# One level of Strassen's scheme in the up-projection of a hybrid decoder step

## The chip, the cores and the metric

The kernel runs on one core of one Trainium2 chip. The metric is the time of one execution on the device, in microseconds (us). A core has five engines that work through their own instruction lists in order and wait for each other by semaphores: TensorE (PE in the profile, with its weight loads as PEld), VectorE (DVE), ScalarE (ACT), GpSimd (POOL) and SyncE (SP), which here issues most DMAs. Matmul results land in eight PSUM banks.

## The reference

One inference step of a decoder layer for 1024 prompt tokens and 64 sample tokens (8 sequences of 8), width 1024, all in float32. A mixer with two branches (a gated linear recurrence and a retention) adds to `x`; then comes the part that the change is in:

```python
    x = x + merged @ w_o
    up = _rmsnorm(x, g_ffn) @ w_up                     # 1024 -> 6144
    upc, conv_ffn_new = _causal_dwconv(up, conv_ffn0, w_ffn_conv, b_ffn_conv)
    gate, val = upc[..., :D_FF], upc[..., D_FF:]       # D_FF = 3072
    x = x + (jax.nn.gelu(gate) * val) @ w_down
    e = _rmsnorm(p.astype(x.dtype) @ w_ple, g_ple)
    x = x + jax.nn.sigmoid(x @ w_ple_gate) * e
```

The convolution has width 3 over time. A last normalisation follows. The outputs are `x` of all tokens and the new states.

## The kernel before, in words

**Halves and units.** The tokens are worked through in two halves, one after the other: the first holds 512 prompt tokens, the second 512 prompt and the 64 sample tokens (576). Rows are kept with channels on partitions and tokens along the free dimension, eight rows of 128 channels for width 1024. The weights of all projections are packed in DRAM as units of 128 x 1024 numbers (512 KB): one unit holds the weights from 1024 inputs to 128 outputs, as eight blocks of 128 x 128. `unit_order` (L58) writes the order of all 330 units by hand; `dense` (L300) and `unit` (L245) run one.

**Two parts.** For precision each operand is split into a float32r part and the exact rest. `block` (L233) does three matmuls for a block: high by high, high by low, low by high; in the second half each of them for two groups of 288 columns, in the first for one of 512. So a unit is 24 matmuls of 512 or 48 of 288. The weights' split is `split_hi` (L224, a cast on ScalarE) and `split_lo` (L228, a subtraction on VectorE); rows are split by `pair` (L306).

**The weight stream.** While unit i runs, its block 0 issues the cast of unit i+2, block 2 the subtraction of i+2, and block 3 the load of unit i+4 by SP (two raw buffers, three buffers for each part).

**Jobs and ticks.** All other work is written as generators. After each block `tick` (L201) advances every job: a job that yields n goes on n ticks later. This fixes the program order of every engine; nothing is reordered later. A result that is asked for with `need` before its job is done makes the job run to its end at once.

**The feed-forward before.** The eight `wo` units add to the residual rows; `j_wo` (L975) splits the rows times `g_ffn` straight away, without the norm. Then for f in 0 to 23 come the up unit of the gate, the up unit of the value and, from f = 4 on, one down unit. The norm of the tokens is found meanwhile by `stat` (L357): sums of squares by small matmuls (L365), a power on GpSimd (L375), a diagonal on VectorE (L380, L390), a broadcast by matmul (L399) and a copy (L400). It is multiplied in when a result is taken out of PSUM (`evac_flat`, L411). `conv` (L436) does one tap on ScalarE (L441) and two on VectorE (L445); then gelu (L991), product (L999) and split. The down units run in groups of four f's: one adds into two residual rows. After the 24 f's come two units of the per-layer embedding (`ple`), whose squares are added up on GpSimd (L354) at once, then the last four down units, then eight gate units and the final normalisation; the second half's input is prepared beside the first half's gate units.

Of the kernel before, what the change touches and what calls it, by code (L numbers as in the profile page):

```python
# [22 lines left out]
RAW = 2  # L23
WIDE = 12
NROW = 70
# [11 lines left out]
# per-channel parameters, one column per 128 channels  # L37
# [4 lines left out]
# constants that depend on shapes alone  # L42
# [15 lines left out]
def unit_order(hf):  # L58
# [8 lines left out]
    for f in range(FF):  # L67
        o += [("up", f), ("up", FF + f)]
        if f >= GRP:
            o.append(("down", f - GRP))  # L70
    o += [("ple", 0), ("ple", 1)]
    o += [("down", f) for f in range(FF - GRP, FF)]
    o += [("gate", m) for m in range(8)] * (1 + hf)
    return o


ORDER = unit_order(0) + unit_order(1)
NU = len(ORDER)
PACKED = unit_order(0)
# [46 lines left out]
class Trunk:  # L126
    def __init__(self, ctx, tc, io):
# [35 lines left out]
        self.cur = 0  # L163
        self.phase = ""
        self.low, self.forced = {}, {}

# [1 line left out]
    def new(self, n=None, dt=F32, wide=False):  # L168
        if n is not None:
            return [self.new(dt=dt, wide=wide) for _ in range(n)]  # L170
        i = (self.wide if wide or not self.free else self.free).popleft()
# [14 lines left out]
    def ps_new(self, n):  # L186
        return [self.banks.popleft() for _ in range(n)]
# [32 lines left out]
    def load(self, i):  # L220
        if i < NU:
            self.nc.sync.dma_start(self.raw[i % RAW], self.io["wpk"][WHERE[ORDER[i]]])

# [21 lines left out]
    def unit(self, H, what, specs, after=None, groups=None):  # L245
        i = self.begin(what)
        for b, (ps, xp, start, stop) in enumerate(specs):
# [5 lines left out]
            if b == 0:  # L253
                self.split_hi(i + 2)
            if b == 2:
                self.split_lo(i + 2)
            if b == 3:
                self.load(i + 4)

    def first_units(self, H, xn, w):  # L260
        """the first two units side by side, at the pace of the arriving input."""
        i = [self.begin(("lx", m)) for m in range(2)]
        ps = [self.ps_new(H.G) for _ in range(2)]
        for k in range(8):
# [4 lines left out]
            if k == 0:  # L269
                self.split_hi(2)  # L270
                self.split_lo(2)
                self.load(4)
            if k == 1:
                self.split_hi(3)
                self.split_lo(3)
                self.load(5)
# [3 lines left out]
    def gates_abreast(self, x2p, groups):  # L280
        """the first two gate units; the block that reads the newest rows comes last in both."""
        i = [self.begin(("gate", m)) for m in range(2)]
        ps = [self.ps_new(len(groups)) for _ in range(2)]
        for m, k in [(m, k) for m in range(2) for k in range(7)] + [(0, 7), (1, 7)]:
# [3 lines left out]
            if m == 0 and k == 0:  # L288
                self.split_hi(i[0] + 2)
            if m == 0 and k == 2:  # L290
                self.split_lo(i[0] + 2)
            if m == 0 and k == 3:
                self.load(i[0] + 4)
            if m == 0 and k == 7:
                self.split_hi(i[1] + 2)
                self.split_lo(i[1] + 2)
                self.load(i[1] + 4)
# [8 lines left out]
    def pair(self, H, row, keep=False):  # L306
        """row -> its float32r part and the exact rest."""
# [34 lines left out]
    def square(self, x, ssum, m, eng=None):  # L342
        """ssum += x * x; with an engine of its own the last square is returned instead."""
# [13 lines left out]
    def stat(self, chunks, ssum, slot, after=None):  # L357
        """1 / sqrt(mean of squares + eps) of every token, on all partitions; ssum: rows to be added up."""
# [52 lines left out]
    def evac_flat(self, H, ps, xf, rb, w):  # L411
        """xf <- ps * rb in the layout of the causal convolution: each sequence after its own prefix."""
# [23 lines left out]
    def conv(self, H, xf, w, wcol, bcol, out=None):  # L436
        """causal depthwise convolution; the last tap writes `out` (compact) when given."""
# [51 lines left out]
    def p0(self, H, xn):  # L489
        """the scaled input in two parts; returns the normalisation of the tokens."""  # L490
# [196 lines left out]
    def back(self, on, h0, np_, t0, ogn):  # L687
        """token-major -> channels on partitions, with the norm's own scale and shift."""
# [16 lines left out]
    def masked_q(self, q, ch, n):  # L705
        """queries of a pair of heads, each with the other's rows at zero."""
# [216 lines left out]
    def branch(self, H, xn, rb, ga, ya, src, lead, m1=None, hook=None):  # L923
        """sigmoid(gate) * projection of src; plus m1 and split when m1 is given."""
# [50 lines left out]
    def j_wo(self, H, ps, x, ssum, m):  # L975
        self.add_ps(H, x, ps)
        yield 1
        p = yield from self.pair_scaled(H, x, self.v("g_ffn", m))
        yield from self.square(x[:, 0:H.T], ssum[:, 0:H.T], m)
        return p  # L980

    def j_up(self, H, u, ps, xf, rb):
        self.evac_flat(H, ps, xf, self.need(rb), 2)
        yield 1
# [9 lines left out]
    def j_val(self, H, up, gate):  # L994
        t, n = yield from up
# [15 lines left out]
    def down(self, H, i, hp, x1):  # L1011
        g, j = divmod(i, GRP)
        ps = [self.ps_new(H.G), self.ps_new(H.G)]
        out = []

        def ev(mi):
            out.append(self.start(self.j_down(H, ps[mi], x1[2 * j + mi], g == FF // GRP - 1)))

        self.unit(
            H, ("down", i), [(ps[mi], hp[GRP * g + kk], kk == 0, kk == 3) for mi in range(2) for kk in range(4)],  # L1020
            {3: lambda: ev(0), 7: lambda: ev(1)},
        )
        if j == GRP - 1:
            for kk in range(GRP):
                self.rel(hp.pop(GRP * g + kk))
        return out

    def j_ple(self, H, ps, e, ssum, m):
        self.act_ps(H, e, ps, AF.Copy)
        yield 1  # L1030
        yield from self.square(e[:, 0:H.T], ssum[:, 0:H.T], m)

    def j_embed(self, H, pe, ssum):
        yield 6
        rb = yield from self.stat(H.chunks, [ssum], H.hf)
        yield 2
        for m in range(8):
            self.nc.vector.scalar_tensor_tensor(
                pe[m][:, 0:H.T], pe[m][:, 0:H.T], self.v("g_ple", m), rb[:, 0:H.T], op0=ALU.mult, op1=ALU.mult
            )  # L1040
            yield 2
# [17 lines left out]
    def j_final(self, H, g, x3, outs, ssum, slot, last):  # L1059
        """the last normalisation of the tokens of g, and the store."""  # L1060
# [29 lines left out]
    def run(self, H, res, nxt):  # L1090
# [17 lines left out]
        # rotary queries and keys  # L1108
# [15 lines left out]
        # values, token-major  # L1124
        self.phase = f"{H.hf} v"
        vt = [self.new(2) for _ in H.chunks]
        for g in range(4):
            banks = self.ps_new(len(H.chunks))
            for j in range(2):
                i = self.begin(("v", 2 * g + j))  # L1130
                wh, wl = (w[i % RING].rearrange("p a b -> p (a b)") for w in (self.whi, self.wlo))
                for c, (t0, nt) in enumerate(H.chunks):
# [9 lines left out]
                    if c == 0:  # L1142
                        self.split_hi(i + 2)
                    if c == 1:
                        self.split_lo(i + 2)
                        self.load(i + 4)
# [6 lines left out]
        # LRU output gate  # L1153
# [12 lines left out]
        # retention beside its gate  # L1166
# [16 lines left out]
        # output projection  # L1183
# [10 lines left out]
        x1p = []  # L1194
        for m in range(8):
            if m + 3 < 8:
                xload(m + 3)
            ps = self.dense(H, ("wo", m), mg)
            x1p.append(self.start(self.j_wo(H, ps, xr[m], ssum, m)))
        x1 = [xr[m] for m in range(8)]  # L1200
        self.rel(mg)

        def stat2():
            yield 7
            for j in x1p:
                self.need(j)
            return (yield from self.stat(H.chunks, [ssum], H.hf))

        rb2 = self.start(stat2())
        # gated convolutional feed-forward  # L1210
        self.phase = f"{H.hf} ffn"
        pp = []
# [8 lines left out]
        hp = {}  # L1221
        gate = None
        for f in range(FF):
            if f == FF - 1:
                pp = [self.start(j_p(kk), delay=kk) for kk in range(2)]
            for s in range(2):
                u = s * FF + f
                xf = self.new(wide=True)
                self.prefix(H, xf, self.stf[:, u], 2)
                ps = self.dense(H, ("up", u), x1p)  # L1230
                up = self.j_up(H, u, ps, xf, rb2)
                late = 8 if f == 0 and s == 0 else 0
                if s == 0:
                    gate = self.start(self.j_gelu(H, up), delay=late)
                else:
                    hp[f] = self.start(self.j_val(H, up, gate), delay=late)
            if f >= GRP:
                self.down(H, f - GRP, hp, x1)
        # per-layer embedding
        self.phase = f"{H.hf} ple"  # L1240
        pe, jp = [], []
        ssum = self.new()
        for j in range(2):
            ps = [self.ps_new(H.G) for _ in range(4)]

            def ev(mi):
                e = self.new()
                pe.append(e)
                jp.append(self.start(self.j_ple(H, ps[mi], e, ssum, 4 * j + mi)))

            self.unit(
                H, ("ple", j), [(ps[mi], pp[kk], kk == 0, kk == 1) for mi in range(4) for kk in range(2)],
                {2 * mi + 1: (lambda mi=mi: ev(mi)) for mi in range(4)},
            )
        self.rel(pp, x1p, rb2)

        emb = self.start(self.j_embed(H, pe, ssum))
# [324 lines left out]
```

## Time and profile before

| | before |
|---|---|
| runs (3) | 2098.27 to 2098.78 us, median 2098.53 |
| span of the profiled execution | 2098.5 us |
| first half's feed-forward, 510.88 to 877.59 | 366.7 us |
| second half's feed-forward, 1568.14 to 2009.30 | 441.2 us |
| granted TensorE clock, mean of the core | 0.996 |
| HBM read, written | 193.95 MB, 7.67 MB |

In the profile's groups a row reads: line of the code, engine, operation, output <- inputs by the program's names, shape, count, then busy us and mean ns of one, then the idle time of the engine just before them and who ended it. In the timeline a row reads start, length, engine, line, operation. In the chain of work in order of time: start, length, engine and line, and how many instructions are merged. The borders of the two stages in the table are where, in that chain, the unbroken TensorE work of the feed-forward begins and ends.

### The profile page before, as it was taken

The page shows a single profiled execution, that of the slowest core. Times are in us where ns is not written, and L with a number is a line of the kernel's source. Part 1 is how long each engine was busy: PE and PEld are TensorE (multiplying, and loading weights), DVE is VectorE, ACT ScalarE, POOL GpSimd, SP SyncE. Part 2 cuts the span into 40 slices and gives each one's busy share as a digit, 9 for nine tenths or more (in the row PEclk, how much of TensorE's full clock was granted, in tenths as well). Part 3 has the DMA queues.
Part 4 walks back from the last instruction along what each step waited for, and adds up shares of the span by engine and source line. Part 5 has one row for each costly group of instructions (what it writes and reads, how often), then busy time and mean ns, then how long its engine had stood idle before and what let it go on. Part 6 is the DMA issues. An engine that isn't in the chain of part 4 may idle for free.

```text
span 2098.5 us, 31597 instructions
## 1 busy us (share of the span) xinstructions
PE 2072.7 (99%) x12862; PEld 1903.0 (91%) x12862; DVE 1274.8 (61%) x1944; ACT 811.0 (39%) x1150; POOL 387.0 (18%) x608
## 2 busy tenths in 40 slices
PE   9999999999999999998999999999999999999997
PEld 7798888888888888888999999989999999999997
DVE  7965345655766666588884433544447556555667
ACT  5654233434433333454463322333234333332354
POOL 4640013102000000234541001440030000000022
PEclk9999999999999999999999999999999999999998
DMA  5333321343333332343332222222322222222234
GB/s 194 98 104 91 101 81 51 101 123 99 100 101 101 91 101 91 111 146 88 117 96 81 83 89 61 94 88 81 116 91 81 84 88 81 81 81 91 84 100 145
DMA packets 64082, 203.67 MB, mean 97 GB/s; under 512 B 7488, under 2 KB 9920, under 8 KB 63936
## 3 DMA queue, kind: packets, MB, share of 16 engines
q1 hardware_dynamic: 63072, 200.97, 31.0%
q8 instruction: 101, 1.65, 0.3%
q10 hardware_dynamic: 864, 0.68, 0.1%
q14 instruction: 45, 0.37, 0.1%
HBM read 193.95 MB, written 7.67 MB: 96 GB/s over the span
## 4 chain that ended last, share of the span: by engine, by line
PE 68%; DVE 4%; issue 2%; ACT 1%; POOL 0%; DMA 0%; DVEq 0%; SPq 0%; ACTq 0%; POOLq 0%
PE bank L237 62%; PE bank L1138 1%; PE bank L1139 1%; PE bank L1137 1%; DVE wlo L231 1%; DVE row L445 0%; DVE row L312 0%; PE bank L883 0%; PE bank L872 0%; DVE row L1053 0%; POOL row L354 0%; PE bank L769 0%; PE bank L767 0%; PE bank L779 0%; PE bank L745 0%
## 5 line engine op out<-in xcount | busy, mean ns | idle before, releaser
L237 PE MATMUL bank<-row,whi 128*128 128x288 f32 (+3 forms) x7360 | 1627.5, 329 | 0.0
L237 PEld LDWEIGHTS bank<-row,whi 128*128 128x128 f32 x7360 | 1185.1, 189 | 97.4 <-issue 0.9
L237 PE MATMUL bank<-row,wlo 128*128 128x288 f32 (+3 forms) x3680 | 1013.4, 327 | 0.8 <-DVE wlo L231 0.7
L237 PEld LDWEIGHTS bank<-row,wlo 128*128 128x128 f32 x3680 | 628.7, 189 | 49.6 <-DVE wlo L231 1.4
L231 DVE TENSOR_TENSOR wlo<-raw,whi 128x1024 fp32r<-128x1024 f32 x330 | 427.1, 1294 | 133.6 <-ACT whi L226 132.3
L226 ACT CAST whi<-raw 128x1024 fp32r<-128x1024 f32 x330 | 344.0, 1042 | 225.6 <-PE bank L237 128.7
L441 ACT ACTIVATE row<-row,vec 128x512 f32<-128x512 f32 (+2 forms) x112 | 95.0, 850 | 397.9 <-DVE row L419 228.9
L445 DVE SCALAR_TENSOR_TENSOR row<-row,vec,row 128x512 f32<-128x512 f32 (+2 forms) x224 | 182.9, 817 | 99.0 <-ACT row L441 95.0
L329 DVE TENSOR_TENSOR row<-bank,row 128x288 f32<-128x288 f32 (+1 forms) x144 | 72.5, 531 | 172.7 <-PE bank L237 172.7
L432 POOL COPY stf<-row 128x2 f32<-128x2 f32 x96 | 18.3, 191 | 740.3 <-DVE row L419 393.6
L354 POOL TENSOR_TENSOR row<-row,row 128x512 f32<-128x512 f32 (+2 forms) x49 | 79.2, 1619 | 359.0 <-ACT row L350 351.0
L310 ACT CAST row<-row 128x512 fp32r<-128x512 f32 (+1 forms) x132 | 84.8, 647 | 150.4 <-DVE row L999 72.6
L312 DVE TENSOR_TENSOR row<-row,row 128x512 fp32r<-128x512 f32 (+1 forms) x132 | 98.1, 745 | 24.1 <-ACT row L310 23.2
L334 DVE TENSOR_TENSOR row<-bank,row 128x288 f32<-128x288 f32 (+1 forms) x168 | 84.0, 528 | 36.2 <-PE bank L237 36.2
L417 DVE TENSOR_TENSOR row<-bank,row 128x288 f32<-128x288 f32 x56 | 25.5, 456 | 113.2 <-PE bank L237 110.6
L415 DVE TENSOR_TENSOR row<-bank,row 128x512 f32<-128x512 f32 x56 | 38.5, 690 | 80.7 <-PE bank L237 78.9
L711 POOL TENSOR_TENSOR row<-row,cst 128x256 f32<-128x256 f32 (+1 forms) x36 | 25.0, 725 | 315.0 <-PE bank L237 315.0
L1138 PE MATMUL bank<-wlo,row 128*128 128x256 f32 (+1 forms) x288 | 81.4, 283 | 0.0
L1139 PE MATMUL bank<-whi,row 128*128 128x256 f32 (+1 forms) x288 | 81.4, 283 | 0.0
L1137 PE MATMUL bank<-whi,row 128*128 128x256 f32 (+1 forms) x288 | 81.4, 282 | 0.0
L909 ACT ACTIVATE row<-row 128x512 f32<-128x512 f32 (+1 forms) x32 | 21.1, 659 | 135.7 <-DVE row L329 135.7
L1137 PEld LDWEIGHTS bank<-whi,row 128*128 128x128 f32 (+1 forms) x288 | 53.3, 185 | 0.0
(156 smaller groups left out, 1418.5 us busy)
## 6 DMA issues: line engine op xcount, KB each, us to landing
raw<-wpk SPq DMA_DIRECT2D x330, 512.0 KB, 3.6
row<-xB SPq DMA_DIRECT2D x16, 288.0 KB, 4.2
row<-xA SPq DMA_DIRECT2D x16, 256.0 KB, 5.3
row<-tabB SPq DMA_DIRECT2D x8, 288.0 KB, 4.7
row<-wri SPq DMA_DIRECT2D x8, 256.0 KB, 5.4
row<-tabA SPq DMA_DIRECT2D x8, 256.0 KB, 4.1
yA<-row SPq DMA_DIRECT2D x8, 256.0 KB, 3.6
row<-s SPq DMA_DIRECT2D x8, 256.0 KB, 6.1
```

Of the source, the lines that this page charges most:

```text
L226: self.nc.scalar.copy(self.whi[i % RING], self.raw[i % RAW])
L231: self.nc.vector.tensor_sub(self.wlo[j], self.raw[i % RAW], self.whi[j].bitcast(F32))
L237: self.nc.tensor.matmul(b[:, 0:g.stop - g.start], lhsT=w, rhs=x[:, g], start=s, stop=e)
L310: nc.scalar.copy(hi[:, 0:H.T], row[:, 0:H.T])
L312: nc.vector.tensor_sub(lo[:, 0:H.T], row[:, 0:H.T], hi[:, 0:H.T].bitcast(F32))
L334: self.nc.vector.tensor_add(row[:, g], b[:, 0:H.n], row[:, g])
L354: (eng or nc.gpsimd).tensor_add(ssum, ssum, s[:, 0:n])
L441: nc.scalar.activation(t[:, 0:n], xf[:, 0:n], AF.Identity, bias=bcol, scale=wcol(0))
L445: nc.vector.scalar_tensor_tensor(t[:, 0:n], xf[:, j:j + n], wcol(j), t[:, 0:n], op0=ALU.mult, op1=ALU.add)
L1137: nc.tensor.matmul(b, lhsT=xh, rhs=wh[:, ws], start=j == 0 and kk == 0, stop=False)
L1138: nc.tensor.matmul(b, lhsT=xh, rhs=wl[:, ws], start=False, stop=False)
L1139: nc.tensor.matmul(b, lhsT=xl, rhs=wh[:, ws], start=False, stop=j == 1 and kk == 3)
```

## The change

The product of the up-projection is cut in two along each dimension, and the eight half-size products become seven. In the weights (A) the first index is gate or value, the second the half of the 1024 inputs; in the rows (B) the first index is the half of the inputs, the second the half of the tokens. The weights' sums are s1 = a21 + a22, s2 = a11 + s1, s3 = a11 + a21, s4 = a12 + s2. The rows' are t1 = b11 - b12, t2 = -t1 - b22, t3 = b22 - b12, t4 = b21 + t2. The signs that this leaves are put right when the products are taken out of PSUM.

- The four sums of weights do not come from the host. During the first half's mixer `make_sums` copies halves of units from DRAM to DRAM by SP and adds to them with accumulating DMAs by GpSimd, four f's at a time.
- The weight stream takes two halves of 128 x 512 as one slot of eight blocks. A product for one f is four blocks, a `step`. There are 84 slots for 24 f's in a half of the tokens where there were 48 units. Three raw buffers now, loads five units ahead.
- `operands` normalises the residual rows first, and splits the rows and their eight differences.
- `step` runs a product and takes its result out of PSUM: products 1 and 2, and 3 and 5, share a bank.
- The first six f's run product by product, all others f by f; 19 of 24 down units run inside the stage and 5 behind it.
- The two embedding units run before the feed-forward; their rows wait in DRAM, and squares and norm of them come beside the last down units.
- `new` and `ps_new` tick the jobs until a row or a bank is free.

```diff
+PRODUCTS = {
+    1: ("a11", "b11"), 2: ("a12", "b21"), 3: ("s4", "b22"), 4: ("a22", "t4"),
+    5: ("s1", "t1"), 6: ("s2", "t2"), 7: ("s3", "t3"),
+}
+def ffn_plan():
+    plan = [("step", f, p) for p in (1, 2, 6, 7, 5, 4, 3) for f in range(LEADP)]      # LEADP = 6
+    steps, down = len(plan), 0
+    for f in range(LEADP, FF):
+        todo = [(f, 1), (f, 6)] + [(f - 1, 3)] * (f > LEADP) + [(f, p) for p in (7, 5, 4, 2)]
+        ready = min(f - 4, down + 2)
+        for i, x in enumerate(todo):
+            plan.append(("step", *x))
+            steps += 1
+            while i >= len(todo) - 2 and steps % 2 == 0 and down < ready:
+                plan.append(("down", down))
+                down += 1
+    plan.append(("step", FF - 1, 3))
...
+    def make_sums(self):
+        yield 30
...
+        for c in range(FF // CHUNK):                                                  # CHUNK = 4
+            for name, base in (("s1", "a21"), ("s3", "a11"), ("s2", "a11"), ("s4", "a12")):
+                nc.sync.dma_start(dst(c, name), src(c, base))
+                yield 7
+            yield 8
+            for name, more in (("s1", "a22"), ("s3", "a21"), ("s2", "s1"), ("s4", "s2")):
+                nc.gpsimd.dma_start(dst(c, name), dst(c, more) if more in SUMS else src(c, more), accum_op=ALU.add)
+                yield 14
+    def hook(self, i, b):
+        if b == 0:
+            self.split_hi(i + 2)
+        if b == 2:
+            self.split_lo(i + 2)
+        if b == 3:
+            self.load(i + 5)
...
+    def operands(self, H, x1, ssum, sq, X, held):
...
+        yield 3
+        rb = yield from self.stat(H.chunks, [ssum] + [r for r in (self.need(j) for j in sq) if r is not None], H.hf)
...
+        def split(row, names):
+            hi, lo = self.new(2, F32R)
+            nc.scalar.copy(hi[:, 0:T], row[:, 0:T])
+            nc.vector.tensor_sub(lo[:, 0:T], row[:, 0:T], hi[:, 0:T].bitcast(F32))
...
+        for k in range(4):
+            norm(k)
+            r = self.new(dt=F32R)
+            nc.scalar.copy(r[:, h1], xn[k][:, h1])
+            nc.vector.tensor_sub(r[:, h2], xn[k][:, h1], r[:, h1].bitcast(F32))
+            yield 0.5
+        for k in range(4, 8):
+            norm(k)
+            split(xn[k], ("b21", "b22"))
+            yield 1
...
+        for k in range(4):
+            t = self.new()
+            nc.vector.tensor_sub(t[:, h1], xn[k][:, h1], xn[k][:, h2])
+            nc.vector.scalar_tensor_tensor(t[:, h2], t[:, h1], -1.0, xn[4 + k][:, h2], op0=ALU.mult, op1=ALU.subtract)
+            split(t, ("t1", "t2"))
+            yield 1
+        for k in range(4):
+            t = self.new()
+            nc.vector.tensor_sub(t[:, h1], xn[4 + k][:, h2], xn[k][:, h2])
+            nc.vector.tensor_add(t[:, h2], xn[4 + k][:, h1], ts[k][:, h2])
+            split(t, ("t3", "t4"))
+            yield 1
...
+    def step(self, H, X, prep, P, f, p):
...
+        for kk in range(4):
+            b = 4 * h + kk
...
+            mm(out, lhsT=wh, rhs=xh, start=first and kk == 0, stop=False, skip_group_check=True)
+            mm(out, lhsT=wh, rhs=xl, start=False, stop=False, skip_group_check=True)
+            mm(out, lhsT=wl, rhs=xh, start=False, stop=kk == 3, skip_group_check=True)
+            if kk % 2:
+                self.tick()
+            self.hook(i, b)
+        if p == 1:
+            nc.scalar.copy(s["row"][:, 0:n], out)
...
+        if p == 2:
+            nc.scalar.copy(s["xg"][:, 2:2 + n], out)
+        elif p == 6:
+            V.tensor_add(r2, out, r1)
+        elif p == 7:
+            V.tensor_add(r1, out, r2)
+        elif p == 5:
+            for o, of in self.second(H, s["xv"], 2):
+                V.scalar_tensor_tensor(o, of(bank), -1.0, of(r1), op0=ALU.mult, op1=ALU.subtract)
+        elif p == 4:
+            V.tensor_sub(s["xv"][:, 2:2 + n], out, r1)
+            s["val"] = self.start(self.j_conv(H, FF + f, s["xv"]), delay=1)
+        else:
+            for o, of in self.second(H, s["xg"], 2):
+                V.tensor_add(o, of(bank), of(r2))
+            gate = self.start(self.j_gelu(H, self.j_conv(H, f, s["xg"])), delay=1)
+            s["hp"] = self.start(self.j_val(H, s["val"], gate), delay=6)
```

In the second half of the tokens the pieces that `second` names are two, the prompt's and the sample's, so those evictions take two instructions.

More of the change, by code (lines that the diff above doesn't have):

```diff
@@ L22 @@
 RING = 3
-RAW = 2
-WIDE = 12
-NROW = 70
+RAW = 3
+WIDE = 16
+NROW = 68
+LEADP = 6
 LEAD_A, LEAD_B = 2, 4
@@ L163, in __init__ @@
         self.cur = 0
+        self.half = None
+        dram = ctx.enter_context(tc.tile_pool(name="sums", bufs=1, space=bass.MemoryType.DRAM))
+        self.sums = [dram.tile([128, CHUNK, len(SUMS), 512], F32, name=f"sums{i}") for i in range(FF // CHUNK)]
+        self.embed = [dram.tile([128, 8, 576], F32, name=f"embed{i}") for i in range(2)]
         self.phase = ""
@@ L170, in new @@
             return [self.new(dt=dt, wide=wide) for _ in range(n)]
+        for _ in range(400):
+            if self.wide or (self.free and not wide):
+                break
+            self.tick()
         i = (self.wide if wide or not self.free else self.free).popleft()
@@ L186, in ps_new @@
     def ps_new(self, n):
+        for _ in range(400):
+            if len(self.banks) >= n:
+                break
+            self.tick()
         return [self.banks.popleft() for _ in range(n)]
@@ L992, in j_gelu, with j_val @@
         return t
-    def j_val(self, H, up, gate):
-        t, n = yield from up
+    def j_val(self, H, val, gate):
+        t, n = self.need(val)
         g = self.need(gate)
@@ L1193, in run @@
         ssum = self.new()
[L1194 to L1212, printed above, removed]
+        sq = []
         srcp = self.io["pA"] if H.hf == 0 else self.io["pB"]
@@ L1219, in j_p @@
             return (yield from self.pair(H, p))
[L1221 to L1238, printed above, removed]
+        pp = [self.start(j_p(kk), delay=8 + kk) for kk in range(2)]
@@ L1257, in run @@
-        emb = self.start(self.j_embed(H, pe, ssum))
+            i = self.begin(("ple", j))
+            for mi in range(4):
+                ps = self.ps_new(H.G)
+                for kk in range(2):
+                    b = 2 * mi + kk
+                    self.block(H.groups, ps, self.whi[i % RING][:, b], self.wlo[i % RING][:, b], self.need(pp[kk]), kk == 0, kk == 1)
+                    self.tick()
+                    self.hook(i, b)
+                self.start(self.j_ple(H, ps, 4 * j + mi))
@@ L1258, in run @@
+        self.rel(pp)
+        self.phase = f"{H.hf} ffn"
+        P = {}
+        for what, *x in PLAN:
+            if what == "step":
+                self.step(H, X, prep, P, *x)
+            else:
+                self.down(H, *x, P, x1)
+        self.rel(held)
+        pe = []
+        emb = self.start(self.j_embed(H, pe))
         x2p = []
-        for f in range(FF - GRP, FF):
-            x2p += self.down(H, f, hp, x1)
+        for d in range(DOWNS, FF):
+            x2p += self.down(H, d, P, x1)
@@ L1358, in main @@
             nc.sync.dma_start(self.stl, io["stl"])
+            self.load(4)
             w_hi(0, 0)
```

230 lines of the change are left out of this document (164 added, 66 removed).

## The prediction

> **What bounds the kernel now.** I read the page first, then the windows and the chain of waits over the two feed-forward stages, then the groups by shape, then the timeline of single operations.
>
> ```profile
> span 2098.5 us, 31597 instructions
> PE 2072.7 (99%) x12862; PEld 1903.0 (91%) x12862; DVE 1274.8 (61%) x1944; ACT 811.0 (39%) x1150; POOL 387.0 (18%) x608
> ```
>
> TensorE is busy for the whole span, so what it does not have to multiply is saved, as long as it is fed. VectorE's 61% is a mean; the stage decides.
>
> ```profile
> 510.88:877.59 366.71, 366.71 (x1616) 302.92 (x1615) 237.01 (x301) 140.98 (x173) 16.07 (x94) 1.00 0.32 98
> 1568.14:2009.30 441.16, 441.16 (x3315) 441.16 (x3315) 269.05 (x464) 156.34 (x194) 39.41 (x193) 1.00 0.27 84
> 940.00:950.00 10.00, 5.65 (x24) 4.05 (x22) 9.07 (x8) 6.65 (x11) 6.36 (x3) 1.00 0.24 59
> 950.00:960.00 10.00, 8.20 (x33) 6.57 (x33) 8.16 (x15) 2.80 (x4) 6.08 (x7) 0.83 0.30 99
> 960.00:970.00 10.00, 10.00 (x61) 9.57 (x61) 3.73 (x5) 2.86 (x5) 1.79 (x2) 0.83 0.37 107
> ```
>
> Columns: stretch, length, busy time of PE, PEld, DVE, ACT, POOL, granted clock, DMA share, GB/s. The first two rows are the feed-forward of the two halves: TensorE never idles, VectorE is busy 65% and 61%. The three others, in the first half's last stage, show what an idle TensorE costs twice: it stands still for 4.35 us, and the next 20 us run at a clock of 0.83.
>
> ```profile
> 510.88 366.71 PE bank L237 x1614
> 1568.14 441.16 PE bank L237 x3312
> ```
> ```profile
> 115.68 0.28 PE L1137 MATMUL bank<-whi,row 128*128 128x256 f32 x1
> ...
> 121.31 0.28 PE L1139 MATMUL bank<-whi,row 128*128 128x256 f32 x1
> ```
>
> The chain in order of time gives the pace of matmuls: 366.71 / 1614 = 0.2272 us at 512 columns, 441.16 / 3312 = 0.1332 us at 288. The value projection shows 256 columns: its first and its 48th matmul are 5.63 us apart, 0.1198 us each. The recorded length (0.28) is not the pace.
>
> **1. Products.** Per f the two up units had 2x8x3 = 48 block matmuls per group of columns; seven products have 7x4x3 = 84 of half the tokens. First half: 48 of 512 columns, 48x0.2272 = 10.91 us, become 84 of 256, 84x0.1198 = 10.06. Second half: 96 of 288 become 84 of 288. Over 24 f: 24x0.85 = 20.2 us, and 24x12x0.1332 = 38.4 us. **Gain 58.6 us.** The first half gets little, since a matmul of 256 columns costs more than half of one of 512.
>
> The Trainium skill ("TensorE: Matmul & The Clock Gate", Back-to-back issue gap) gives columns / 2.4 + 2.5 ns, 109 and 216 ns for these two; by it, as an estimate, the first half would gain 28 us and the sum below would be 8 us lower. The rows measure both shapes in this kernel and are slower, so they are used.
>
> **2. Weight halves.** 14 half units a f make 3.5 slots of eight blocks where there were 2 units, so 36 more slots a half of tokens, each with one cast (ScalarE) and one subtraction (VectorE).
>
> ```profile
> L231 DVE TENSOR_TENSOR wlo<-raw,whi 128x1024 fp32r<-128x1024 f32 x330 | 427.1, 1294 | 133.6 <-ACT whi L226 132.3
> L445 DVE SCALAR_TENSOR_TENSOR row<-row,vec,row 128x512 f32<-128x512 f32 x112 | 89.4, 799 | 46.0 <-ACT row L441 44.0
> L445 DVE SCALAR_TENSOR_TENSOR row<-row,vec,row 128x592 f32<-128x592 f32 x96 | 80.0, 835 | 47.5 <-ACT row L441 45.8
> L312 DVE TENSOR_TENSOR row<-row,row 128x576 fp32r<-128x576 f32 x66 | 52.4, 795 | 12.0 <-ACT row L310 11.7
> L312 DVE TENSOR_TENSOR row<-row,row 128x512 fp32r<-128x512 f32 x66 | 45.8, 695 | 12.1 <-ACT row L310 11.5
> L334 DVE TENSOR_TENSOR row<-bank,row 128x288 f32<-128x288 f32 x112 | 45.7, 449 | 20.8 <-PE bank L237 20.8
> L310 ACT CAST row<-row 128x576 fp32r<-128x576 f32 x66 | 44.2, 674 | 72.8 <-DVE row L999 39.8 <-DVE row L334 18.8 <-DVE row L918 5.6
> L310 ACT CAST row<-row 128x512 fp32r<-128x512 f32 x66 | 40.7, 621 | 77.6 <-DVE row L999 32.8 <-DVE row L448 17.3 <-DVE row L334 17.1
> L334 DVE TENSOR_TENSOR row<-bank,row 128x512 f32<-128x512 f32 x56 | 38.3, 684 | 15.4 <-PE bank L237 15.4
> L1038 DVE SCALAR_TENSOR_TENSOR row<-row,vec,row 128x576 f32<-128x576 f32 x8 | 6.5, 810 | 0.0
> L1038 DVE SCALAR_TENSOR_TENSOR row<-row,vec,row 128x512 f32<-128x512 f32 x8 | 6.0, 745 | 0.0
> L350 ACT ACTIVATE row<-row 128x256 f32<-128x256 f32 x7 | 2.9, 415 | 5.0 <-DVE row L1054 5.0
> L354 DVE TENSOR_TENSOR row<-row,row 128x256 f32<-128x256 f32 x6 | 2.5, 423 | 2.1 <-ACT row L350 2.1
> ```
> ```profile
> 706.98 1.22 DVE L231 TENSOR_TENSOR wlo<-raw,whi 128x1024 fp32r<-128x1024 f32 x1
> 708.12 0.69 DVE L334 TENSOR_TENSOR row<-bank,row 128x512 f32<-128x512 f32 x1
> 708.72 0.68 DVE L312 TENSOR_TENSOR row<-row,row 128x512 fp32r<-128x512 f32 x1
> ```
>
> Back to back, VectorE starts the next instruction 0.09 us before the record of the last ends (706.98 to 708.12 is 1.14, not 1.22), so an instruction costs its length less 0.09. A plain step of f in the first half is then 4.5 subtractions x 1.14, five evictions of 256 columns (0.33, between the 288 and 512 rows), four convolution taps (0.71), product, split and two adds (0.60 each): 12.0 us of VectorE against 10.06 + 24x0.2272 = 15.5 of TensorE (second half 13 against 17.6). The middle of the stage is still TensorE's. Its two ends are not.
>
> **3. The start of the stage: the normalised operands.** Before, the matmuls ran on unnormalised rows and the eviction multiplied. Now nothing starts before the norm, and only the two embedding units cover it. They tick once a block; the job's waits put the sums of squares at tick 4, the diagonal at 7, the broadcast at 11.
>
> ```profile
> 504.44 1.05 PE bank L365 x8
> ...
> 510.42 0.47 PE bank L399 x2
> ```
> ```profile
> 1560.57 0.99 PE bank L365 x10
> ...
> 1567.34 0.80 PE bank L399 x4
> ```
>
> The sums are now of two rows, so L365 doubles to 2.1 and 2.0 us: **+2.0** in all. First half, from the start of the embedding units: 11 blocks of 0.68, 2.1, L399 and its copy 1.2: norm at 10.8 us; units done at 16x0.68 + 2.1 + 0.5 = 13.5. Second: 12.4 and 15.6.
>
> Every tick from 11 to 24 then issues operand work, eight rows to normalise and split and eight differences. In each, VectorE's subtraction stands right behind ScalarE's cast of the same row, so VectorE, in order, waits for it (0.04 to pass on). First half: four rows of b11 0.75 + 0.42 + 0.42 + 0.08 - 0.09 = 1.57; four of b2x 0.75 + 0.62 + 0.70 + 0.08 - 0.09 = 2.05; eight differences 0.42 + 0.45 (a fused one at 256, estimate from L354 and L1038) + 0.62 + 0.70 - 0.10 = 2.1. Sum 31.3 us. What is queued behind: each slot's subtraction, issued two slots ahead by program order. That of slot 2 stands behind nine rows of this, slot 3 behind thirteen, slot 4 behind all. So slot 4's weights are ready at 10.8 + 31.3 + 4x1.14 = 46.7 us, while TensorE by then has 13.5 and four slots of 24x0.1198 = 2.88, 25.0 us: a stall of 21.5 (0.24 of slot 4 runs first). Second half, same sum at 576 and 288: 1.70, 2.27 and 2.33 give 34.5; 12.4 + 34.5 + 4.6 = 51.5 against 15.6 + 4x3.2 = 28.4: 22.8. **Cost 44.3 us.** Bounds: without the waits for ScalarE the rows cost 0.99, 1.26 and 1.29 (second 1.09, 1.43, 1.47), and the stalls are 9.5 and 10.2, 19.7 in all; above, embedding evictions of 0.6 each between the casts add 5. I take the upper figure since nothing stands between cast and subtraction.
>
> These idle pieces are 5 to 7 us long, and the rows at 950 lost 20x0.17 = 3.4 us after one of 4.35. Most of a slow clock hides under VectorE; the last slot's does not: 2.5 a half, **+5** (0 to 7). The Trainium skill (same page, Why this matters for your kernels) says to leave no gap over about 3 us; the trace agrees.
>
> **4. The lead's end.** Six f's finish products 4 and 3 together, so twelve convolutions fall on six slots of TensorE. VectorE per slot, first half: 1.14 + two evictions 0.66 + two convolutions 2x1.45 = 4.7 for slots 16 to 18, then with products and splits 5.3, 6.5, 6.8, against 2.88. The subtraction for two slots on may be late by two slots before TensorE stops. Adding up, it is late by 0.3 at slot 20, 2.1, 4.6, 8.2 and 11.2 at slot 24, after which two down units (2x5.45 of TensorE, 4.8 of VectorE) win it back. Second half, per slot 5.0, 5.0, 5.1, 5.9, 7.3, 7.5 against 3.2: 11.7. **Cost 22.9** (0, if the queue's order lets it drain, to 30). ScalarE's casts in these slots sum to about the same, but follow VectorE.
>
> **5. Moves.** The embedding units cost the same earlier. Their squares (POOL, L354) now run beside five downs: L365 may wait for POOL, 1 us a half, **+2** (-3 to +8; the stall of 4.35 us above lies next to it and may shift). The base copies go through SP ahead of weight loads, the accumulating ones through POOL, which waits for each to land.
>
> ```profile
> q1 hardware_dynamic: 63072, 200.97, 31.0%
> raw<-wpk SPq DMA_DIRECT2D x330, 512.0 KB, 3.6
> ```
>
> 31% of the DMA engines moved 97 GB/s, so all move some 313. A chunk's four copies (4 MB in 28 ticks, 19 us) beside 1.9 MB of weights need 18.8 us: just enough. A load now has 2.6 units, 14.2 us, less 3.6 to land: 10.6 to spare. I take nothing, for that spare hides it; 0 to +50 with the rival below. No gain is possible here. The sums are issued by tick 30 + 6x92 = 582, their use begins at 656.
>
> **Sum.** The span is the profiled execution's own time and equals the median (2098.53) within 0.1. 2098.5 - 58.6 + 44.3 + 2.0 + 5 + 22.9 + 2 = **2116 us**.
>
> **Rivals.** (a) Faster: VectorE's queue is not the wall. If the operand rows cost only their busy time and the lead's convolutions drain into the downs, 2098.5 - 58.6 + 19.7 + 2 + 2.5 = 2064 us. It decides where an operand row takes under 1.4 us. For it: VectorE has 35% free in the stage. Against: program order. (b) One end only: the lead's convolutions drain, the operands do not: 2116 - 23 = 2093. (c) The copies starve the mixer's weights. If a byte from DRAM to DRAM costs two, six chunks need (8 + 1.9) / 0.313 = 31.6 us for 19 + 10.6, 2 late each: 2128; at 2.5 it is 2166. It decides at 1.85. For it: the bursts fill the engines. (d) The change does not save the products: excluded, the 256-column pace is in the trace.
>
> **Numbers.** Forecast 0.46, (a) 0.30, (b) 0.12, (c) 0.12. Forecast alone: 2102 to 2132, from the bounds of 4 and the clock. The range 2060 to 2138 takes in (a) and half of (c). A difference of 0.2% (4.2 us) is what can be told. Faster: (a) and half of (b), 0.36; same: the rest of (b) and the forecast's edge, 0.08; slower 0.56.
>
> **What would show it.** Right: behind each embedding stage three idle pieces of TensorE of 5 to 7 us ending on wlo, with VectorE alternating with ScalarE; two more shorter stalls on wlo 50 us later; clock under 1 there; middle of the stage at 15.5 and 17.6 us a f without waits; mixer of the first half unchanged. Wrong: TensorE unbroken behind the embedding, or waits for raw or POOL before it.

## The result, and the profile after

| | before | after |
|---|---|---|
| median of 4 runs each | 2098.46 us | 2125.43 us |
| lowest to highest | 2098.27 to 2098.78 | 2124.10 to 2125.81 |
| ratio, 95% interval | | 1.0128 (1.0114 to 1.0143) |
| span of the profiled execution | 2098.5 us | 2124.0 us |
| granted TensorE clock, mean | 0.996 | 0.982 |

The kernel is slower by 27.0 us, 9.4 more than the forecast of 2116, on the side forecast and inside the range. Between the two profiled spans it is 25.5 us.

The page of the changed kernel, to be read against the first rows of the prediction:

```profile
span 2124.0 us, 34118 instructions
PE 2046.8 (96%) x13456; PEld 1912.2 (90%) x13456; DVE 1418.7 (67%) x2176; ACT 919.6 (43%) x1334; POOL 445.5 (21%) x630
```

TensorE has less to do in spite of its slower clock (2046.8 us for 2072.7), but no longer does it without a break: 77 us of the span are idle, where 26 were.

Windows of the first half's feed-forward (stretch, length, busy time of PE, PEld, DVE, ACT, POOL, granted clock, DMA share, GB/s):

```profile
513.93:555.00 41.07, 27.47 (x145) 24.99 (x144) 27.55 (x44) 18.90 (x35) 0.00 (x0) 0.75 0.29 96
555.00:590.00 35.00, 34.12 (x282) 33.74 (x281) 25.06 (x39) 15.35 (x17) 1.11 (x6) 1.00 0.54 177
590.00:619.00 29.00, 21.73 (x156) 20.92 (x155) 28.65 (x44) 19.54 (x27) 4.39 (x7) 0.89 0.30 97
619.01:895.65 276.64, 276.64 (x1896) 258.19 (x1895) 220.01 (x313) 140.11 (x185) 25.75 (x70) 1.00 0.47 151
655.77:686.87 31.10, 31.10 (x218) 29.17 (x217) 24.76 (x36) 15.86 (x21) 2.84 (x9) 1.00 0.48 153
1751.57:1786.59 35.02, 35.02 (x267) 35.02 (x266) 27.13 (x47) 16.49 (x21) 4.24 (x17) 1.00 0.43 136
```

The lead is the first six f's, which run product by product. The first row is the stall behind the embedding units: TensorE stands for 13.6 of 41 us and runs the rest at a clock of 0.75, while VectorE, busy 67%, is not full either. That is how two engines look that wait for each other. In the third, the lead's end, VectorE is full (28.65 of 29.00). The fourth is the rest of the stage, without a gap. The last two are two f's each in the middle of the halves: 15.55 and 17.51 us a f.

TensorE's timeline in the stall, the operations with a wait of 0.4 us or more ahead of them (in brackets the wait and who ended it; L1156 to L1158 are the three matmuls of a step's block, L323 the cast and L328 the subtraction of the weights):

```profile
516.91 0.50 PE L1156 MATMUL bank<-row,whi 128*128 128x256 f32 x1 [1.73 <-ACT row L1094]
527.89 0.39 PE L1156 MATMUL bank<-row,whi 128*128 128x256 f32 x1 [2.00 <-ACT whi L323]
530.50 0.45 PE L1158 MATMUL bank<-row,wlo 128*128 128x256 f32 x1 [2.10 <-DVE wlo L328]
537.54 0.58 PE L1156 MATMUL bank<-row,whi 128*128 128x256 f32 x1 [2.66 <-ACT whi L323]
540.28 0.58 PE L1158 MATMUL bank<-row,wlo 128*128 128x256 f32 x1 [1.94 <-DVE wlo L328]
547.02 0.39 PE L1156 MATMUL bank<-row,whi 128*128 128x256 f32 x1 [2.08 <-ACT whi L323]
548.28 0.58 PE L1158 MATMUL bank<-row,wlo 128*128 128x256 f32 x1 [0.76 <-DVE wlo L328]
```

Three slots, 10 us apart, come late. Each is waited for twice: for its high part, which was not forecast, and two matmuls later for its low part.

VectorE's timeline, inside the stall:

```profile
520.88 0.75 DVE L1078 SCALAR_TENSOR_TENSOR row<-row,vec,row 128x512 f32<-128x512 f32 x1
522.36 0.69 DVE L1086 TENSOR_TENSOR row<-row,row 128x512 fp32r<-128x512 f32 x1 [0.74 <-ACT row L1085]
522.97 0.75 DVE L1078 SCALAR_TENSOR_TENSOR row<-row,vec,row 128x512 f32<-128x512 f32 x1
```

A row takes 522.97 - 520.88 = 2.09 us (2.05 forecast), of which VectorE idles 0.74 until ScalarE has cast the row.

TensorE's timeline at the lead's end, the operations with a wait of 1 us or more:

```profile
601.54 0.39 PE L1158 MATMUL bank<-row,wlo 128*128 128x256 f32 x1 [1.40 <-DVE wlo L328]
606.84 0.39 PE L1158 MATMUL bank<-row,wlo 128*128 128x256 f32 x1 [2.16 <-DVE wlo L328]
613.95 0.58 PE L1158 MATMUL bank<-row,wlo 128*128 128x256 f32 x1 [3.28 <-DVE wlo L328]
```

All three are for the low part of the weights.

### The profile page after: what moved, and what is told of

Its sections match the earlier page's. It is cut to its first block, busy times and chain, and to the rows that moved or that the text cites. A ratio compares the mean times of both kernels' runs of the same rounds, so it can differ in the third digit from the quotient of the medians.

```text
span 2124.0 us, 34118 instructions
## 1 busy us (share of the span) xinstructions
PE 2046.8 (96%) x13456; PEld 1912.2 (90%) x13456; DVE 1418.7 (67%) x2176; ACT 919.6 (43%) x1334; POOL 445.5 (21%) x630
## 4 chain that ended last, share of the span: by engine, by line
PE 79%; DVE 13%; issue 3%; ACT 3%; DMA 1%; POOL 1%; SPq 0%; DVEq 0%; ACTq 0%; POOLq 0%
PE bank L334 49%; PE bank L1158 7%; PE bank L1157 7%; PE bank L1156 7%; DVE wlo L328 3%; DVE row L532 2%; PE bank L1366 2%; PE bank L1367 2%; PE bank L1365 2%; DVE row L399 1%; ACT whi L323 1%; ACT row L1085 1%; PE bank L854 1%; PE bank L866 1%; PE bank L832 1%
## 5 line engine op out<-in xcount | busy, mean ns | idle before, releaser
L334 PE MATMUL bank<-row,whi 128*128 128x288 f32 (+3 forms) x5056 | 1126.2, 330 | 1.5 <-ACT whi L323 1.0
L334 PEld LDWEIGHTS bank<-row,whi 128*128 128x128 f32 x5056 | 815.8, 189 | 68.2 <-ACT whi L323 1.4
L334 PE MATMUL bank<-row,wlo 128*128 128x288 f32 (+3 forms) x2528 | 700.2, 328 | 4.0 <-DVE wlo L328 4.0
L328 DVE TENSOR_TENSOR wlo<-raw,whi 128x1024 fp32r<-128x1024 f32 x402 | 518.5, 1291 | 191.1 <-ACT whi L323 190.5
L323 ACT CAST whi<-raw 128x1024 fp32r<-128x1024 f32 x402 | 420.0, 1046 | 351.0 <-issue 122.8
L334 PEld LDWEIGHTS bank<-row,wlo 128*128 128x128 f32 x2528 | 434.4, 189 | 39.2 <-DVE wlo L328 5.4
L1158 PE MATMUL bank<-row,wlo 128*128 128x256 f32 (+1 forms) x1344 | 397.7, 296 | 23.7 <-DVE wlo L328 23.7
L1156 PE MATMUL bank<-row,whi 128*128 128x256 f32 (+1 forms) x1344 | 397.9, 296 | 21.8 <-ACT whi L323 16.3
L1157 PE MATMUL bank<-row,whi 128*128 128x256 f32 (+1 forms) x1344 | 397.0, 295 | 0.2
L1158 PEld LDWEIGHTS bank<-row,wlo 128*128 128x128 f32 x1344 | 263.2, 196 | 26.6 <-DVE wlo L328 26.6
L1156 PEld LDWEIGHTS bank<-row,whi 128*128 128x128 f32 x1344 | 263.0, 196 | 26.0 <-ACT whi L323 17.9
L1157 PEld LDWEIGHTS bank<-row,whi 128*128 128x128 f32 x1344 | 263.2, 196 | 2.0 <-DVE row L1095 1.3
L519 POOL COPY stf<-row 128x2 f32<-128x2 f32 x96 | 47.2, 492 | 742.7 <-DVE row L1191 450.3
L421 DVE TENSOR_TENSOR row<-bank,row 128x288 f32<-128x288 f32 (+1 forms) x168 | 81.0, 527 | 29.3 <-PE bank L334 29.3
L1367 PE MATMUL bank<-whi,row 128*128 128x256 f32 (+1 forms) x288 | 81.3, 282 | 0.0
```

What stands on the lines that cost most here:

```text
L323: self.nc.scalar.copy(self.whi[i % RING], self.raw[i % RAW])
L328: self.nc.vector.tensor_sub(self.wlo[j], self.raw[i % RAW], self.whi[j].bitcast(F32))
L334: self.nc.tensor.matmul(b[:, 0:g.stop - g.start], lhsT=w, rhs=x[:, g], start=s, stop=e)
L1156: mm(out, lhsT=wh, rhs=xh, start=first and kk == 0, stop=False, skip_group_check=True)
L1157: mm(out, lhsT=wh, rhs=xl, start=False, stop=False, skip_group_check=True)
L1158: mm(out, lhsT=wl, rhs=xh, start=False, stop=kk == 3, skip_group_check=True)
```

## The experiments

The theory: the loss is VectorE's program order at two places, the operand rows that each wait for a cast, and the lead's convolutions bunched at its end. Rivals: the sum of VectorE's work, whatever its order; the clock; the copies for the sums of weights. Medians are compared with the kernel before on the same chip: 2097.97 us (19 runs) for the first four experiments, 2098.28 (13) for the next four, 2098.50 (7) for the last two. The experiments without an interval are one run each, and runs of the kernel before on one chip lie up to 3.3 us apart.

**1. The cast one row ahead.** In `operands` each subtraction is issued one row later, so ScalarE has had a whole row's time for the cast.

```diff
+        rest = deque()
             nc.scalar.copy(hi[:, 0:T], row[:, 0:T])
-            nc.vector.tensor_sub(lo[:, 0:T], row[:, 0:T], hi[:, 0:T].bitcast(F32))
+            def low():
+                nc.vector.tensor_sub(lo[:, 0:T], row[:, 0:T], hi[:, 0:T].bitcast(F32))
...
+            rest.append(low)
...
+        def late():
+            while len(rest) > 1:
+                rest.popleft()()
```

> Only the order inside the operand work is changed: the subtraction of a row is issued one row later, so that ScalarE's cast of it has VectorE's next row to hide under. Theory (VectorE's in-order wait for the cast is what makes an operand row cost 1.6 to 2.1 us): a row falls to its busy time, 1.0 to 1.5 us, the stall behind the embedding units from 21.5 to about 9.5 us in the first half and from 22.8 to about 10.2 in the second, so 24 us less: 2101 us. Rival (VectorE's load or the weights' arrival sets the stall, the waits lie beside it): within 5 us of the changed kernel, 2120 to 2126.

Measured: 2098.17 us (10 runs), ratio to before 1.0002 (0.9993 to 1.0012), 27 us under the changed kernel. No operation was removed; what went is the wait for the cast, with what it brings along. VectorE's timeline:

```profile
517.15 0.75 DVE L1079 SCALAR_TENSOR_TENSOR row<-row,vec,row 128x512 f32<-128x512 f32 x1
517.81 0.69 DVE L1089 TENSOR_TENSOR row<-row,row 128x512 fp32r<-128x512 f32 x1
518.42 0.75 DVE L1079 SCALAR_TENSOR_TENSOR row<-row,vec,row 128x512 f32<-128x512 f32 x1
```

A row now takes 518.42 - 517.15 = 1.27 us, without a wait. Of the 29.3 us between the two profiled spans, 19.8 are idle time of TensorE. The other 9.5 are busy time, for the same matmuls at a mean clock of 0.988 instead of 0.982; 1.6 of the 29.3 arise before the value projection, where the clock held in this execution (see experiment 5). TensorE's waits, summed, are shorter for both parts of the weights; first the changed kernel, then this one (L1180 and L1178 stand for L1158 and L1156):

```profile
PE bank L1158 <- DVE wlo L328: 23.7, 12, 3.3
PE bank L1156 <- ACT whi L323: 16.3, 7, 4.4
```
```profile
PE bank L1180 <- DVE wlo L328: 16.9, 12, 3.1
PE bank L1178 <- ACT whi L323: 6.2, 4, 2.7
```

**2. The rows spread out.** From the fifth row on a row comes every third tick instead of every tick; the order inside a row stays.

```diff
-            yield 1
+            yield 3
```

> Only the yields of the operand work are changed: three ticks instead of one between rows from the fifth on, so that fewer of them stand ahead of each slot's weight subtraction. Theory (program order makes the weights of slots 2 to 4 wait behind all operand rows, but a row still costs 2.1 us): the stall then ends where the last row is needed, at product 7: about 15 us in each half instead of 21.5 and 22.8, so 14 us less, 2111. Rival (the order does not matter, the sum of the work does): 2122 to 2126.

Measured: 2104.88 us, 20.5 under the changed kernel, more than expected. So it is not VectorE's total that stops TensorE there: the same work, thinned out, lets the weights through.

**3. Both.**

> Both edits together. Theory: rows at their busy time and in step with the slots leave 2 to 3 us of stall in each half, so 39 us less than the changed kernel, and most of the loss of clock (5 us) goes too: 2081 to 2087 us, faster than the kernel before. Rival (VectorE's load in the lead is the bound): above 2100.

Measured: 2095.72 us (10 runs), ratio 0.9990 (0.9981 to 0.9999). A miss, 9 us above the expected range: the two gains do not add. VectorE's timeline shows a wait for the weights' cast that recurs with the slots (13 times from 513 to 600 us, 10.6 us in all), and ScalarE's shows why:

```profile
532.48 0.68 DVE L1089 TENSOR_TENSOR row<-row,row 128x512 fp32r<-128x512 f32 x1
534.47 1.23 DVE L328 TENSOR_TENSOR wlo<-raw,whi 128x1024 fp32r<-128x1024 f32 x1 [1.31 <-ACT whi L323]
```
```profile
532.60 0.62 ACT L1086 CAST row<-row 128x512 fp32r<-128x512 f32 x1 [1.81 <-DVE row L1126]
533.13 0.37 ACT L1194 COPY row<-bank 128x256 f32<-128x256 f32 x1
533.39 1.05 ACT L323 CAST whi<-raw 128x1024 fp32r<-128x1024 f32 x1
```

ScalarE waits 1.81 us for VectorE's difference row, with the cast of the weights queued behind that; VectorE then waits 1.31 us for this cast, with the next rows queued behind that. Block 0 issues the cast and block 2 the subtraction, too close together when an operand row falls between.

**4. The lead without its taps.**

```diff
-        for j in range(1, w + 1):
+        for j in range(1, w + 1) if taps else ():
```

> The changed kernel with the two VectorE taps of the twelve convolutions of the first six f's left out in each half of the tokens (so part of the convolution is not computed). Theory (the convolutions that pile up at the lead's end cost 11.2 and 11.7 us): 23 us less, 2102. Rival (ScalarE's casts or the banks bound that stretch): less than 8 us off, above 2117.

Measured: 2105.45 us, 20.0 under the changed kernel, against 22.9 forecast for the pile-up. The lead's convolutions do stop TensorE.

**5. No sums of weights.** Each sum is replaced by the half `a11` as it lies in DRAM.

```diff
         if name in SUMS:
-            return self.sums[f // CHUNK][:, f % CHUNK, SUMS.index(name), :]
+            name = "a11"
-            self.start(self.make_sums())
```

> The changed kernel without the DMAs that form the sums of weights (the up-projection then takes a plain half in place of each sum, so it computes something else). Theory (these DMAs hide under the mixer): the embedding units of the first half begin within 0.5 us of where they begin in the changed kernel (500.95 us), and the time stays at 2123 to 2126. Rival (copies and accumulations delay weights or GpSimd's work in the mixer): they begin 1.5 us earlier, where the kernel before has the same point, and the time falls by 1.5 us or more.

Measured: 2122.86 us, 2.6 under the changed kernel, which for one run is within the spread of runs; the trace tells more. The embedding units start 2.2 us sooner, and the rival's 1.5 was nearer. But the sums do not starve the mixer. Windows from the first value-projection matmul to the embedding units, before and after:

```profile
115.68:499.40 383.72, 383.72 (x1954) 327.75 (x1953) 199.14 (x294) 141.08 (x215) 70.37 (x62) 1.00 0.31 94
```
```profile
117.34:500.95 383.61, 383.59 (x1954) 327.87 (x1953) 198.46 (x289) 137.75 (x210) 89.61 (x81) 1.00 0.77 205
```

With the DMA engines busy 77% instead of 31%, the 384 us are the same to 0.1. The loss lies before 117 us. VectorE's groups there, 67 to 73 us, two convolution taps, first without sums and then in the changed kernel, and what GpSimd ran beside them in the latter:

```profile
L532 DVE SCALAR_TENSOR_TENSOR row<-row,vec,row 128x512 f32<-128x512 f32 x2 | 3.3, 1670 | 0.2 <-ACT row L528 0.2
```
```profile
L532 DVE SCALAR_TENSOR_TENSOR row<-row,vec,row 128x512 f32<-128x512 f32 x2 | 4.3, 2166 | 0.2 <-ACT row L528 0.2
```
```profile
69.25 1.40 POOL L309 DMA_DIRECT2D sums<-wpk  x1
70.17 1.82 POOL L643 TENSOR_TENSOR row<-row,row 128x512 f32<-128x512 f32 x1
```

The first accumulating DMA's issue occupies GpSimd for about 1 us (its next instruction starts 0.92 us later), and VectorE's two taps beside GpSimd's work, slow already without it, take 1.0 us more. TensorE then waits 1.10 us at 74.04 as well as 1.18 at 75.73, and behind these two the clock falls in some executions and not in others. Windows of the changed kernel and of experiment 1, which has the same program up to there:

```profile
75.00:80.00 5.00, 4.27 (x12) 3.41 (x13) 4.18 (x6) 2.10 (x4) 1.52 (x2) 0.67 0.80 200
```
```profile
75.00:80.00 5.00, 4.29 (x19) 3.56 (x20) 4.19 (x6) 2.09 (x4) 1.50 (x2) 1.00 0.80 197
```

At 0.67 there are 12 matmuls in the 5 us, at full clock 19. The value projection starts at 117.34 us in the first, 115.74 in the second, 115.14 without sums. So the sums cost 0.6 us, or 2.2 where the clock falls.

**6. The weights' subtraction later.** Experiment 3, and in the lead the subtraction of a slot's weights at block 6 and the load at block 7.

```diff
-        if b == 2:
+        if b == (6 if self.lead else 2):
             self.split_lo(i + 2)
-        if b == 3:
+        if b == (7 if self.lead else 3):
             self.load(i + 5)
...
+                    self.lead = LEADP not in P and x[0] < LEADP
```

> The third experiment's kernel, and in the lead's slots the weights' subtraction is issued at block 6 instead of 2 (the load behind it at block 7). Theory (ScalarE and VectorE wait for each other in turn there: the weights' cast stands behind an operand's cast that waits for VectorE, and VectorE's subtraction waits 1.3 us for that cast): about seven such waits a half go, 10 to 14 us less than the third experiment, 2082 to 2086. Rival (VectorE's load is the bound): within 3 us of 2095.7.

Measured: 2077.99 us (4 runs), ratio 0.9905 (0.9890 to 0.9920), 17.7 us under experiment 3, more than expected. The mutual wait is confirmed: from 513 to 600 us VectorE waits 0.3 us for the weights' cast, where it waited 10.6 in experiment 3.

**7. A lead of four f's.** Experiment 6 with `LEADP = 4`.

> The kernel of e6 with four f's in the lead instead of six. Theory: eight convolutions pile up instead of twelve (5 us less a half), but the operands have 30.8 us of products 1, 2 and 6 to hide under instead of 39.4 (5 us more a half): within 5 us of e6. Rival (the pile-up is the larger cost): 8 us or more under e6.

Measured: 2094.93 us (10 runs), ratio 0.9983 (0.9974 to 0.9993). A miss: 17 us more. A short lead has fewer convolutions, but TensorE now comes to rows that are not ready (the second line below; experiment 6 has no such wait, and 13.3 us of the first):

```profile
PE bank L1181 <- DVE wlo L329: 14.2, 14, 2.5
PE bank L1180 <- DVE row L1090: 11.6, 12, 1.9
```

**8. The lead's convolutions spread.** Experiment 6, and the lead takes products 1, 2 and 6 for all six f's first, then 7, 5, 4 and 3 f by f, so a convolution falls due every other step.

```diff
-    plan = [("step", f, p) for p in (1, 2, 6, 7, 5, 4, 3) for f in range(LEADP)]
+    plan = [("step", f, p) for p in (1, 2, 6) for f in range(LEADP)]
+    plan += [("step", f, p) for f in range(LEADP) for p in (7, 5, 4, 3)]
```

> The kernel of e6 with the lead's products 7, 5, 4, 3 done f by f instead of product by product, so that the twelve convolutions lie beside 24 steps of TensorE instead of 12. Theory (pile-up of VectorE's work): per f 7.7 us of VectorE on 5.75 of TensorE instead of 4.7 to 6.8 on 2.9 a slot; the stall falls from 11 to some 6 us a half, 9 to 11 us under e6. Rival (the total of VectorE's work to the end of the lead counts, not its order): within 3 us of e6.

Measured: 2076.50 us (4 runs), ratio 0.9896 (0.9881 to 0.9910), only 1.5 under experiment 6; the rival holds. Its waits and a window of it:

```profile
PE bank L1180 <- DVE row L1208: 16.7, 11, 2.6
```
```profile
575.00:590.00 15.00, 11.47 (x93) 11.27 (x94) 14.89 (x23) 9.47 (x13) 3.67 (x6) 1.00 0.43 139
```

L1208 takes product 5 out of its bank. VectorE is full (14.89 of 15.00 us): for this change of order it is the sum of its work that counts.

**9. Product 6 f by f too.**

```diff
-    plan = [("step", f, p) for p in (1, 2, 6) for f in range(LEADP)]
-    plan += [("step", f, p) for f in range(LEADP) for p in (7, 5, 4, 3)]
+    plan = [("step", f, p) for p in (1, 2) for f in range(LEADP)]
+    plan += [("step", f, p) for f in range(LEADP) for p in (6, 7, 5, 4, 3)]
```

> The kernel of e8 with product 6 taken into the f-by-f part of the lead too. Theory (what is left of the loss there is the sum of VectorE's work up to the lead's end, 100% busy in e8's trace, so its order no longer matters): within 3 us of e8's 2076.5. Rival (density still counts: 8.6 us of VectorE on 7.2 of TensorE per f instead of 7.7 on 5.75): 5 to 8 us under e8.

Measured: 2086.70 us (4 runs), ratio 0.9942 (0.9928 to 0.9957): a miss, 10 us more than experiment 8. The products that need the last operand rows now come sooner, and a wait for these appears (the second line). From 513 to 555 us the clock is 0.92, where it was 1.00 in experiment 8; so this order does count:

```profile
PE bank L1180 <- DVE row L1208: 12.4, 9, 1.8
PE bank L1181 <- DVE row L1091: 7.1, 8, 1.3
```

**10. The lead's gelu products later.** Experiment 8, with `j_val`, which multiplies gate and value and splits them, put off in the lead.

```diff
-            s["hp"] = self.start(self.j_val(H, s["val"], gate), delay=6)
+            s["hp"] = self.start(self.j_val(H, s["val"], gate), delay=42 - 6 * f if f < LEADP else 6)
```

> The kernel of e8 with the gate-by-value products and splits of the first six f's (1.2 us of VectorE each) put off until the seventh f, where the two down units leave VectorE free. Theory (the sum of VectorE's work up to the lead's end is the bound): 7 us of work leave the lead, 5 to 7 us less in each half, 2063 to 2067. Rival (the work only comes back as a stall of the down units that need the products): within 3 us of e8.

Measured: 2075.59 us (4 runs), ratio 0.9890 (0.9873 to 0.9906), within 1 us of experiment 8. The work comes back a little later as a wait of the down units for split rows (L401), which in experiment 8 was 3.4 us:

```profile
PE bank L1180 <- DVE row L1208: 9.8, 11, 1.0
PE bank L336 <- DVE row L401: 8.2, 11, 1.8
```

## Why the prediction was right, and where it was short

**Products: right.** 15.55 and 17.51 us a f, against 15.5 and 17.6 forecast, without a wait. The 256-column pace measured in the value projection was the right price.

**The start of the stage: right.** The norm was there 10.4 us behind the embedding units' start (10.8 forecast), and slot 4's low weights at 47.3 us (46.7). Experiments 1 and 2 undo most of the stall in two ways that leave VectorE's work as it is. What the working missed is that ScalarE is held too: the casts of the weights stand behind row casts that wait for VectorE, hence the waits for `whi`. So each of the three idle pieces, forecast as one of 5 to 7 us on wlo, is a pair, together 4.1, 4.6 and 2.8 us, and slow matmuls fill the rest. This did not alter the sum, since VectorE's queue was the slower of the two.

**The lead's end: right in place and nearly in size.** 20.0 us of the 22.9 went with the taps in experiment 4. TensorE stops three times there on wlo, where two were named. From the start of the embedding units to the first down unit the changed kernel needs 118.1 us in the first half, of which 13.5 + 24x2.875 = 82.5 are TensorE's work (24 slots come before that unit): 35.6 lost, against 21.5 + 2.5 + 11.2 = 35.2 forecast. In the second half 131.6 less 15.6 and 24x3.2 = 76.7: 39.3, against 37.0.

**The clock: right that it falls** (0.75 in the stall). Of the 35.6 us lost, 21.7 are idle time and 13.8 busy time beyond the 82.5, at a mean clock of 0.89 there. How much of the 13.8 would have been lost to VectorE's queue at full clock, no run shows, so the +5 is not measured by itself. The stall of 4.35 us that it was read from is two in the trace of before: 0.73 us for wlo at 941.13, and 3.74 for GpSimd (L354) at 950.12.

**Rivals.** (a), that VectorE's queue is not the wall, fell for this kernel. Experiments 1, 2 and 6 show that at the start of the stage it was the order, which can be changed, that made it the wall. At the lead's end other orders (experiments 8 to 10) gained 2.4 us at most on experiment 6, one lost 9, and VectorE is full there (14.89 of 15.00 us in experiment 8). (b) fell with experiment 4. (c) fell: the mixer behind the first value projection took the same time with 2.2 times the bytes. The 313 GB/s that its price used are not borne out: there 77% of the DMA engines moved 205, which makes 266 for all.

**The step that was short is 5, the moves,** put at +2. Between spans the forecast was +17.5 and 25.5 was measured, 8.0 more. Of this 1.6 us arise before the value projection of the first half. Another 5.3 are in the first half from the embedding units to the next half's input: +22.3 where the terms make +17.0. Of these, 0.4 are the lead's and 0.5 the middle's: the 276.64 us of the stage without a gap hold 1440 matmuls of 256 columns and 456 of 512, 276.1 by the paces of the prediction. The other 4.4 lie behind the stage's last product, where the trace of before already had a stall. Windows from there (before: from the end of the unbroken work) to the next half's input, before and after:

```profile
877.59:968.60 91.01, 84.17 (x381) 69.55 (x380) 67.35 (x81) 48.15 (x72) 36.30 (x24) 0.96 0.39 124
```
```profile
895.65:992.50 96.85, 87.19 (x384) 70.29 (x382) 76.72 (x90) 48.58 (x73) 37.77 (x26) 0.95 0.43 144
```

TensorE's idle time grew from 6.8 to 9.7 us, and what the slow clock takes (length times one less the clock, rounded as shown) from 3.6 to 4.8: 4 together, where +1 had been put. The prediction saw the place ("may shift") and neither the size nor the wait. TensorE's waits in these two windows, before and after (the wait, its total, times, longest):

```profile
PE bank L365 <- POOL row L354: 4.4, 2, 3.7
PE bank L237 <- DVE wlo L231: 0.7, 1, 0.7
```
```profile
PE bank L334 <- DVE wlo L328: 2.8, 2, 2.5
PE bank L452 <- POOL row L441: 2.3, 2, 1.4
PE bank L334 <- ACT whi L323: 1.0, 1, 1.0
```

The wait for GpSimd's squares, which the term was put down for, fell from 4.4 to 2.3 us. The waits for the weights grew from 0.7 to 3.8, and those for the diagonals of the norms from 1.7 to 3.3. Why the weights came later there was not tried. That the embedding's norm runs there explains little: in the kernel before its sums of squares already lay in this stretch (887.81, after a wait of 0.69 us; now at 916.32, after 1.39). Some 1.4 us of the first half's surplus (4.4 - 3) stay without a place. The rest of the 8.0 is 1.0 in the second half and its mixer, the balance of 2.3 more up to its first down unit and of less elsewhere.

Last, 1.4 us lie between the changed kernel's span and its median. Wherever the record has both for one execution, its time is 1.7 to 2.2 us above its span. By that the span of 2098.5 before belongs to an execution some 1.8 us slower than the median, and that the two are equal, as the prediction notes, is a coincidence.

## What to carry to other kernels

A cast on one engine and a subtraction on another, issued back to back for each row, run two in-order queues in lockstep: here a row took 2.09 us instead of 1.27, and issuing the subtraction one row later took 27 us off a kernel of 2125. What counts is what is queued behind the wait: the weights for TensorE. A saving of matmuls should therefore be entered together with the extra vector work at the stage's two ends, where it comes in a burst; with operands and weight splits put in another order (experiments 8 and 10) the same seven products gave 2076 us, 1.0 to 1.1% under the kernel before.

## What the runs showed of the hardware

- Behind two gaps of TensorE of 1.1 and 1.2 us (74.04 and 75.73), less than 2 us apart, the granted clock was 0.66 to 0.74 (75 to 80 us) in six of the ten profiled executions with this program up to there, among them the changed kernel's. Behind the same gaps it stayed at 1.00 in the other four, experiment 1's among them, so what decides is not shown. The Trainium skill ("TensorE: Matmul & The Clock Gate", Why this matters for your kernels) warns of gaps over about 3 us; here the clock also fell behind shorter ones, and the measurement decides.
- VectorE's taps were longer beside GpSimd: 1.67 us each beside its vector work and 2.17 with a DMA issue in it, against a mean of 0.81 over all 112 of this shape in the changed kernel. The Trainium skill ("GPSIMD Engine Reference", Specifications) says that GpSimd shares its way to SBUF with VectorE instructions of two inputs from there; the trace agrees for the vector work, and the page says nothing of the issue.
- Accumulating 1 MB in DRAM took half as long again as copying it, from issue to landing:

```profile
sums<-wpk SPq DMA_DIRECT2D x24, 1024.0 KB, 8.8
sums<-wpk POOLq DMA_DIRECT2D x12, 1024.0 KB, 12.8
sums<-sums POOLq DMA_DIRECT2D x12, 1024.0 KB, 13.9
```
